# Gate and up products of one feed-forward, computed in two halves of the array's rows

## The chip, the cores and the metric

The kernel runs on one core of a Trainium2 chip. TensorE multiplies matrices on an array of 128 rows by 128 columns: one operand (the weights of the array, up to 128 x 128) is loaded, the other streams through, and the products are added into a bank of PSUM (128 partitions x 512 fp32). VectorE and ScalarE read PSUM and work on data in SBUF; GpSimd does a few small things; SyncE issues the transfers from HBM. The metric is device time in microseconds (us) of one execution.

## The reference

A trunk of two layers works on 256 tokens of 1,024 features, in fp32. Each layer is a feed-forward, a token mixer that runs in parallel with a cross-attention, and a second feed-forward, each followed by a layer norm over `alpha * x + sublayer(x)`:

```python
for l in range(DEPTH):
    x = layer_norm(alpha * x + 0.5 * swiglu(x, ffn_w_gate[l, 0], ...), ...)
    ...                                    # mixer and cross-attention
    x = layer_norm(alpha * x + mix, ln_g[l, 1], ln_b[l, 1])
    x = layer_norm(alpha * x + 0.5 * swiglu(x, ffn_w_gate[l, 1], ...), ...)

def swiglu(x, w_gate, w_up, w_down):
    return (jax.nn.silu(x @ w_gate) * (x @ w_up)) @ w_down
```

The hidden width is 2,816. So there are four feed-forwards; the change concerns the second one, that is the one that ends the first layer: l = 0, j = 1 in the code.

## The kernel before

Every fp32 operand of a large product is split into a high and a low part of type fp32r (a shorter float that TensorE takes in one pass): `split` (L101, L102) copies the raw weights to `wh` on ScalarE and subtracts on VectorE to get `wl`. A product is then three matmuls: high by high, high by low, low by high.

A feed-forward (`ffn`) goes through 11 groups of 256 hidden features. The weights of a group's gate and up matrices come in two pieces of 128 x 2048, each with 4 of the 8 chunks `k` of 128 input features; per chunk there are 256 gate columns and then 256 up columns. All four feed-forwards but the first do the first two groups in another way than the rest (`xs_groups` = 2):

- `gu_xs` (groups 0 and 1, once for each half `t` of the tokens): the activations are the loaded operand and the weights stream, 512 columns at a time. For each of 8 chunks `mm3` (L183, L184, L185) adds three matmuls into one bank `gx`. Silu on ScalarE and a multiplication on VectorE read the bank; the result is transposed by `hx` (L355) and split into the high and low `h`. During the second call, after chunk 5, the eight transposes `xt` of the layer norm ahead (`pending`) are issued, which the second half of the tokens needs.
- `gu_ws` (groups 2 to 10): the weights are the loaded operand and the activations stream. For each half `fc` of a group and each of gate and up (`m`) a bank `gu` is filled by `mmw` (L191): per chunk, `wh` with high and low activations in one matmul of 512 columns (two halves of the bank), and `wl` with the high ones in a matmul of 256. `comb` (L195, L196) then adds the two halves of the bank with a copy on ScalarE and an add on VectorE; Silu (L322), the multiplication (L323) and the split into `h` (L326, L327) follow.

The third step is `down`: `mm3` with `h` loaded and the down weights streaming, into the four banks `y`. The down product of group g - 1 stands behind the gate and up products of group g; after group 2 come those of groups 0 and 1 together; those of groups 8, 9 and 10 stand at the end, in `tail`, because the layer norm follows there by halves.

PSUM has eight banks. Four go to `y` (and other long sums), four rotate for all the rest (`mbank`): gate and up products, transposes `xt` and `hx`. A bank is given out in the order of the program, the fourth after a given one is the same bank again, and a matmul into it waits until its last reader is done.

The transfers stand on SyncE's queue in the order of the list `pieces`, three raw buffers ahead at most, and five pairs of `wh`, `wl` exist. Engines take their instructions in the order in which they are laid out, which follows the program with some matmuls moved.

Elsewhere the kernel has matmuls on part of the array: the scores of the cross-attention (`sc`, L485) work on 64 rows each, two of them one after the other with different rows and banks, in plain fp32. The projections `qkp` (L448 to L450) are fp32r matmuls of the whole array with 256 columns.

Of the kernel before, what the change touches and what calls it, by code (L numbers as in the profile page):

```python
# [8 lines left out]
F32 = mybir.dt.float32  # L9
F32R = mybir.dt.float32r  # L10
AF = mybir.ActivationFunctionType
ALU = mybir.AluOpType
AX = mybir.AxisListType

P = 128
T = 256
D = 1024
KC = D // P
# [13 lines left out]
def trunk(ctx: ExitStack, tc: tile.TileContext, d, out):  # L32
    nc = tc.nc
    pe, act, dve, pool = nc.tensor, nc.scalar, nc.vector, nc.gpsimd
# [3 lines left out]
    wp = ctx.enter_context(tc.tile_pool(name="wp", bufs=5))  # L38
# [9 lines left out]
    def ybank(name):  # L48
        return psy.tile([P, 512], F32, tag="y", name=name)

    def mbank(name):
        return psm.tile([P, 512], F32, tag="mm", name=name)

    def tmp(name):
        return tp.tile([P, 512], F32, tag="t", name=name)
# [4 lines left out]
    def downs_after(g, xs):  # L60

        if g < max(xs, 1) or g > NG - TAIL:
            return []
        return list(range(g)) if g == xs else [g - 1]
# [74 lines left out]
    def get(*key):  # L139
        while state["next"] < len(pieces) and state["next"] <= state["used"] + 1:  # L140
            trace_piece()
        assert pieces[state["used"]][0] == key, (pieces[state["used"]][0], key)
        state["used"] += 1
        return made.pop(key)
# [16 lines left out]
    for k in range(KC):  # L161
        q, o = (k, 0) if k < 2 else (1 + k // 2, k % 2 * CH)
        nc.sync.dma_start(xw[q][:, o:o + CH], d["xw"][:, k * CH:(k + 1) * CH])
        h, l = first[k // 4]
        s = slice((k % 4) * 512, (k % 4) * 512 + 512)
        split_act(xw[q][:, o:o + T], x0, k, 1)
        split(xw[q][:, o + T:o + CH], h[:, s], l[:, s])
    cur = {"x": x0}
# [10 lines left out]
    def mm3(o, a, b, start, stop):  # L179

        ah, al = a
        bh, bl = b
        pe.matmul(o, ah, bh, start=start, stop=False)  # L183
        pe.matmul(o, ah, bl, start=False, stop=False)  # L184
        pe.matmul(o, al, bh, start=False, stop=stop)  # L185

    def mmw(bank, w, a, k):

        for part in ((0, 1), (1, 0))[k % 2]:
            o, b = (bank[:, :T], a[:, 0]) if part else (bank, a.rearrange("p c t -> p (c t)"))  # L190
            pe.matmul(o, w[part], b, start=(k, part) == (0, 0), stop=(k, part) == (KC - 1, 0))  # L191

    def comb(o, bank):

        act.activation(o, bank[:, T:], AF.Copy)  # L195
        dve.tensor_add(o, o, bank[:, :T])  # L196

    HALVES = (slice(0, 64), slice(64, 128))
# [6 lines left out]
    def tsl(t):  # L205
        return slice(t * P, (t + 1) * P)

    def xpart(k, t):
        return cur["x"][:, k, 0, tsl(t)], cur["x"][:, k, 1, tsl(t)]
# [79 lines left out]
    def ffn(l, j, xs_groups, i, last=False):  # L289
        hT = {}  # L290
        y = {}

        def new_h(g):
            hT[g] = hp.tile([P, 2, 2, T], F32R, tag="h", name=f"h{l}{j}_{g}")

        def gu_ws(g, outer=False):
            w = [get("gu", l, j, g, 0), get("gu", l, j, g, 1)]
            new_h(g)
            banks = {}

            def mm(fc, m, k):
                if k == 0:
                    bank = ybank if outer and g == 0 else mbank
                    banks[fc, m] = bank(f"gu{l}{j}_{g}_{fc}{m}")
                c0 = (k % 4) * 512 + m * 256 + fc * P
                wk = w[k // 4]
                mmw(banks[fc, m], (wk[0][:, c0:c0 + P], wk[1][:, c0:c0 + P]), cur["x"][:, k], k)

            if outer:
                for k in range(KC):  # L310
                    for fc in range(2):
                        for m in range(2):
                            mm(fc, m, k)
            for fc in range(2):
                t_ = tmp(f"s{l}{j}_{g}_{fc}")
                for m in range(2):
                    if not outer:
                        for k in range(KC):
                            mm(fc, m, k)
                    comb(t_[:, m * 256:(m + 1) * 256], banks[fc, m])  # L320
                    if m == 0:
                        act.activation(t_[:, :256], t_[:, :256], AF.Silu)  # L322
                dve.scalar_tensor_tensor(t_[:, 256:], t_[:, :256], 0.5, t_[:, 256:],  # L323
                                         op0=ALU.mult, op1=ALU.mult)
                hh = hT[g][:, 0, fc, :]
                act.activation(hh, t_[:, 256:], AF.Copy)  # L326
                dve.tensor_sub(hT[g][:, 1, fc, :], t_[:, 256:], hh.bitcast(F32))  # L327

        xsw = {}

        def gu_xs(g, t, mid=None):
            if t == 0:
                xsw[g] = [get("gu", l, j, g, 0), get("gu", l, j, g, 1)]
                new_h(g)
            w = xsw[g]
            b = mbank(f"gx{l}{j}_{g}_{t}")
            for k in range(KC):
                wk = w[k // 4]
                s = slice((k % 4) * 512, (k % 4) * 512 + 512)
                mm3(b, xpart(k, t), (wk[0][:, s], wk[1][:, s]), k == 0, k == KC - 1)  # L340
                if k == 5 and mid:
                    mid()
            t_ = tmp(f"sx{l}{j}_{g}_{t}")
            act.activation(t_[:, :256], b[:, :256], AF.Silu)
            dve.scalar_tensor_tensor(t_[:, 256:], t_[:, :256], 0.5, b[:, 256:],
                                     op0=ALU.mult, op1=ALU.mult)

            def rest():
                hx(g, t, t_)
            return rest  # L350

        def hx(g, t, t_):
            tb = mbank(f"hx{l}{j}_{g}_{t}")
            for fc in range(2):
                pe.transpose(tb[:, fc * P:(fc + 1) * P], t_[:, 256 + fc * P:256 + (fc + 1) * P], ident)  # L355
            tv = tb[:, :256].rearrange("p (c t) -> p c t", c=2)
            hh = hT[g][:, 0, :, tsl(t)]
            act.activation(hh, tv, AF.Copy)
            dve.tensor_sub(hT[g][:, 1, :, tsl(t)], tv, hh.bitcast(F32))

        def down(g, t, hs, w):
            for fc in range(2):
                a = (hT[g][:, 0, fc, tsl(t)], hT[g][:, 1, fc, tsl(t)])
                for h in hs:
                    if (t, h) not in y:
                        y[t, h] = ybank(f"y{l}{j}_{t}{h}")
                    s = slice(fc * D + 512 * h, fc * D + 512 * h + 512)
                    mm3(y[t, h], a, (w[0][:, s], w[1][:, s]), g == 0 and fc == 0,
                        g == NG - 1 and fc == 1)

        late = []
        for t in range(2):
            for g in range(xs_groups):
                late.append(gu_xs(g, t, pending if (t, g) == (0, xs_groups - 1) else None))
                if len(late) > 2:
                    late.pop(0)()
                    late.pop(0)()
        for g in range(NG):
            if g == 2:
                if i == 0:  # L380
                    late_loads()
                gb = load_ln(i)
            if g >= xs_groups:
                gu_ws(g, outer=(l, j) == (0, 0) and g < 2)
                while late:
                    late.pop(0)()
            for q in downs_after(g, xs_groups):
                w = get("wd", l, j, q)
                for t in range(2):
                    down(q, t, (0, 1), w)  # L390
        nx = None if last else new_act(f"x{i}")
        ws = {g: get("wd", l, j, g) for g in range(NG - TAIL, NG)}

        def tail(t):
            for h in range(2):
                if last and (t, h) == (1, 1):
                    break
                for g in range(NG - TAIL, NG):
                    down(g, t, (h,), ws[g])
                ln_half(i, t, h, y[t, h])  # L400
            else:
                return
            down(NG - TAIL, t, (1,), ws[NG - TAIL])
            y2 = mbank("ylast")[:, :256]
            ends = [(g, fc) for g in range(NG - TAIL + 1, NG) for fc in range(2)]
            for q, o in enumerate((y[1, 1][:, :256], y2)):
                for n, (g, fc) in enumerate(ends):
                    s = slice(fc * D + 512 + 256 * q, fc * D + 768 + 256 * q)
                    mm3(o, (hT[g][:, 0, fc, tsl(t)], hT[g][:, 1, fc, tsl(t)]),
                        (ws[g][0][:, s], ws[g][1][:, s]), (q, n) == (1, 0), n == len(ends) - 1)  # L410
            ln_close(i, t, y[1, 1], y2)
        norm_both(i, gb, nx, tail)
# [420 lines left out]
    o = OutProj(0, mix, 1)  # L833
# [63 lines left out]
```

## Time and profile before

| | us |
|---|---|
| median of 3 runs (987.28 to 988.73) | 988.04 |
| the profiled execution | 987.03 |
| its span, first to last instruction | 984.9 |
| TensorE busy with matmuls in the span | 973.0 |
| VectorE busy | 663.1 |
| ScalarE busy | 528.8 |
| granted clock of TensorE, mean | 0.996 |

In rows of single instructions the columns are the start in us from the span's begin, the length in us, the engine, the line of the kernel, the operation, the tile written and the tiles read, the shape and the count; a row with a count above one goes from the first start to the last end. Shapes such as 64*128 are rows by columns of the array that are used, and 64x256 the streamed operand. A matmul's length goes from its start to its last result, so that successive matmuls overlap: the pace is read from start to start. PEld is the load of weights.

### The profile page before, as it was taken

Reading aid. Unit: us, or ns where it says so; the run is one execution under the profiler, and the core shown is the slowest. Engines: PE = TensorE matmul, PEld = TensorE weight load, DVE = VectorE, ACT = ScalarE, POOL = GpSimd, SP = SyncE. Lnnn points to the kernel's source line nnn. Section 1 sums busy time; section 2 is a strip of 40 time slices with the busy share of each in tenths; the row PEclk is TensorE's granted clock in tenths of the full one; section 3 lists DMA queues with packets and bytes.
Section 4 is the critical chain, followed back from the end, with each engine's and each line's share of the span. In section 5 each row is a group of like instructions: output and inputs, shape, how many; then the busy total and the mean of one; then the engine's idle time right before and its main releaser. Section 6 shows DMA issues by size and latency. Waiting matters only on the chain.

```text
span 984.9 us, 13270 instructions
## 1 busy us (share of the span) xinstructions
PE 973.0 (99%) x5276; PEld 832.0 (84%) x5276; DVE 663.1 (67%) x1013; ACT 528.8 (54%) x847; POOL 20.0 (2%) x31
## 2 busy tenths in 40 slices
PE   9999999999999999999999999999989999999997
PEld 8888888888888888888888888889988788888885
DVE  7676566868677656565865656577877687556565
ACT  7565555457535555555355555535874346455550
POOL 0000000000000000000000000001000000000000
PEclk9999999999999999999999999999999999999999
DMA  9784646466435654645474545434734446546421
GB/s 323 282 316 152 226 155 231 167 231 221 173 132 203 236 202 155 230 148 194 171 257 171 209 177 202 173 113 163 265 111 151 179 159 239 202 158 218 168 86 43
DMA packets 28141, 186.91 MB, mean 190 GB/s; under 512 B 3504, under 2 KB 3504, under 8 KB 7216
## 3 DMA queue, kind: packets, MB, share of 16 engines
q1 hardware_dynamic: 27792, 185.55, 52.4%
q8 instruction: 41, 0.67, 0.3%
q10 hardware_dynamic: 288, 0.52, 0.1%
q14 instruction: 20, 0.16, 0.0%
HBM read 185.01 MB, written 1.05 MB: 189 GB/s over the span
## 4 chain that ended last, share of the span: by engine, by line
PE 95%; DVE 2%; ACT 1%; DMA 1%; issue 1%; SPq 0%; DVEq 0%; ACTq 0%
PE gu L191 43%; PE y L183 8%; PE y L185 8%; PE y L184 8%; PE gx L183 2%; PE gx L185 2%; PE gx L184 2%; PE cb L191 2%; PE cx L191 2%; PE cg L191 2%; PE yo L183 2%; PE yo L185 1%; PE yo L184 1%; PE kb L191 1%; PE xt L255 1%; PE qkp L448 1%
## 5 line engine op out<-in xcount | busy, mean ns | idle before, releaser
L102 DVE TENSOR_TENSOR wl<-raw,wh 128x1024 fp32r<-128x1024 f32 x334 | 395.0, 1208 | 145.8 <-ACT wh L101 144.7
L191 PE MATMUL gu<-x,wh 128*128 128x512 f32 x1216 | 389.0, 395 | 0.0
L101 ACT ACTIVATE wh<-raw 128x1024 fp32r<-128x1024 f32 x334 | 332.8, 1042 | 97.2 <-PE y L185 28.8
L191 PEld LDWEIGHTS gu<-x,wl 128*128 128x128 f32 x1216 | 228.4, 188 | 52.3 <-DVE wl L102 1.0
L191 PE MATMUL gu<-x,wl 128*128 128x256 f32 x1216 | 243.0, 278 | 0.2 <-DVE wl L102 0.2
L191 PEld LDWEIGHTS gu<-x,wh 128*128 128x128 f32 x1216 | 189.5, 189 | 3.6 <-ACT wh L101 0.2
L183 PE MATMUL y<-wh,h 128*128 128x512 f32 (+1 forms) x352 | 137.4, 390 | 0.0
L184 PE MATMUL y<-wl,h 128*128 128x512 f32 (+1 forms) x352 | 136.6, 388 | 0.0
L185 PE MATMUL y<-wh,h 128*128 128x512 f32 (+1 forms) x352 | 136.5, 389 | 0.0
L196 DVE TENSOR_TENSOR s<-s,gu 128x256 f32<-128x256 f32 x152 | 63.1, 418 | 103.2 <-ACT s L195 103.0
L195 ACT ACTIVATE s<-gu 128x256 f32<-128x256 f32 x152 | 57.9, 382 | 104.6 <-PE gu L191 104.5
L185 PEld LDWEIGHTS y<-wh,h 128*128 128x128 f32 x352 | 66.1, 188 | 14.2 <-DVE h L327 0.4
L184 PEld LDWEIGHTS y<-wl,h 128*128 128x128 f32 x352 | 66.1, 188 | 13.6
L183 PEld LDWEIGHTS y<-wh,h 128*128 128x128 f32 x352 | 66.1, 188 | 12.9 <-ACT h L326 0.7
L326 ACT ACTIVATE h<-s 128x256 fp32r<-128x256 f32 x76 | 31.8, 418 | 66.1 <-DVE s L323 65.9
L322 ACT ACTIVATE s<-s 128x256 f32<-128x256 f32 x76 | 31.5, 416 | 37.9 <-DVE s L196 37.9
L327 DVE TENSOR_TENSOR h<-s,h 128x256 fp32r<-128x256 f32 x76 | 32.1, 422 | 17.2 <-ACT h L326 17.0
L285 ACT ACTIVATE x<-xt 128x512 fp32r<-128x512 f32 x20 | 11.4, 597 | 51.5 <-PE xt L255 51.1
L183 PE MATMUL gx<-wh,x 128*128 128x512 f32 x96 | 38.0, 396 | 0.0
L185 PE MATMUL gx<-wh,x 128*128 128x512 f32 x96 | 37.5, 392 | 0.0
L184 PE MATMUL gx<-wl,x 128*128 128x512 f32 x96 | 37.4, 390 | 0.0
L323 DVE SCALAR_TENSOR_TENSOR s<-s 128x256 f32<-128x256 f32 x76 | 32.0, 421 | 1.8 <-ACT s L322 0.5
(218 smaller groups left out, 988.9 us busy)
## 6 DMA issues: line engine op xcount, KB each, us to landing
raw<-in_wgu SPq DMA_DIRECT2D x83, 1024.0 KB, 4.8
raw<-in_wd SPq DMA_DIRECT2D x43, 1024.0 KB, 4.8
raw<-in_wconv SPq DMA_DIRECT2D x10, 1024.0 KB, 5.3
raw<-in_wout SPq DMA_DIRECT2D x8, 1024.0 KB, 4.8
raw<-in_wm SPq DMA_DIRECT2D x7, 1024.0 KB, 5.0
gb<-in_lngb SPq DMA_DIRECT2D x6, 1024.0 KB, 4.8
raw<-in_wkv SPq DMA_DIRECT2D x4, 1024.0 KB, 4.7
raw<-in_wop SPq DMA_DIRECT2D x4, 776.0 KB, 4.2
```

Source lines behind the costliest of these rows:

```text
L101: act.activation(h, raw, AF.Copy)
L102: dve.tensor_sub(l, raw, h.bitcast(F32))
L183: pe.matmul(o, ah, bh, start=start, stop=False)
L184: pe.matmul(o, ah, bl, start=False, stop=False)
L185: pe.matmul(o, al, bh, start=False, stop=stop)
L191: pe.matmul(o, w[part], b, start=(k, part) == (0, 0), stop=(k, part) == (KC - 1, 0))
L195: act.activation(o, bank[:, T:], AF.Copy)
L196: dve.tensor_add(o, o, bank[:, :T])
L322: act.activation(t_[:, :256], t_[:, :256], AF.Silu)
L323: dve.scalar_tensor_tensor(t_[:, 256:], t_[:, :256], 0.5, t_[:, 256:], op0=ALU.mult, op1=ALU.mult)
L326: act.activation(hh, t_[:, 256:], AF.Copy)
L327: dve.tensor_sub(hT[g][:, 1, fc, :], t_[:, 256:], hh.bitcast(F32))
```

## The change

In the second feed-forward alone, each matmul of the gate and up products is replaced by two, one for the upper 64 rows of the array (input features 0 to 63 of the chunk) and one for the lower 64, which add into two different banks. The two banks are added afterwards: ScalarE copies one of them to SBUF, VectorE adds the other.

In groups 2 to 10 the three products (wh by high x, wh by low x, wl by high x) are matmuls of 256 columns each, and all three add into the same 256 columns, so that gate and up of a half group stand side by side in one bank: 48 matmuls of 64 rows and 256 columns where 16 matmuls of 128 rows, half of 512 and half of 256 columns, stood. The copy and the add are of 512 columns, once per half group, in place of 256 columns each, twice. In groups 0 and 1 each of the 24 matmuls of 512 columns becomes two with 64 rows, and a second bank, a copy and an add of 512 columns come in.

```diff
+        def gu_rows(g):
+
+            w = [get("gu", l, j, g, 0), get("gu", l, j, g, 1)]
+            new_h(g)
+            for fc in range(2):
+                t_ = tmp(f"s{l}{j}_{g}_{fc}")
+                ab = [mbank(f"gr{l}{j}_{g}_{fc}{r}") for r in range(2)]
+                for m in range(2):
+                    for k in range(KC):
+                        c0 = (k % 4) * 512 + m * 256 + fc * P
+                        wk = w[k // 4]
+                        for n, (wp, xp) in enumerate(((0, 0), (0, 1), (1, 0))):
+                            for o, r in zip(ab, HALVES):
+                                pe.matmul(o[:, m * 256:(m + 1) * 256], wk[wp][r, c0:c0 + P],
+                                          cur["x"][r, k, xp], start=(k, n) == (0, 0),
+                                          stop=(k, n) == (KC - 1, 2))
+                act.activation(t_, ab[1], AF.Copy)
+                dve.tensor_add(t_, t_, ab[0])
+                act.activation(t_[:, :256], t_[:, :256], AF.Silu)
+                dve.scalar_tensor_tensor(t_[:, 256:], t_[:, :256], 0.5, t_[:, 256:],
+                                         op0=ALU.mult, op1=ALU.mult)
+                hh = hT[g][:, 0, fc, :]
+                act.activation(hh, t_[:, 256:], AF.Copy)
+                dve.tensor_sub(hT[g][:, 1, fc, :], t_[:, 256:], hh.bitcast(F32))
+
         def gu_ws(g, outer=False):
+            if (l, j) == (0, 1):
+                return gu_rows(g)
...
+            rows = (l, j) == (0, 1)
             b = mbank(f"gx{l}{j}_{g}_{t}")
+            b2 = mbank(f"gy{l}{j}_{g}_{t}") if rows else None
...
-                mm3(b, xpart(k, t), (wk[0][:, s], wk[1][:, s]), k == 0, k == KC - 1)
+                if rows:
+                    for n, (xp, wp) in enumerate(((0, 0), (0, 1), (1, 0))):
+                        for o, r in zip((b, b2), HALVES):
+                            pe.matmul(o, xpart(k, t)[xp][r], wk[wp][r, s], start=(k, n) == (0, 0),
+                                      stop=(k, n) == (KC - 1, 2))
+                else:
+                    mm3(b, xpart(k, t), (wk[0][:, s], wk[1][:, s]), k == 0, k == KC - 1)
...
             t_ = tmp(f"sx{l}{j}_{g}_{t}")
+            if rows:
+                act.activation(t_, b2, AF.Copy)
+                dve.tensor_add(t_, t_, b)
+                b = t_
```

`HALVES` is `(slice(0, 64), slice(64, 128))`.

## The prediction

> **What bounds the kernel now.** I read the page first, then the clock by core, then the chain of waits over the stage that changes (298 to 466 us), then single matmuls in order of time.
>
> ```profile
> PE   9999999999999999999999999999989999999997
> PEclk9999999999999999999999999999999999999999
> PE 95%; DVE 2%; ACT 1%; DMA 1%; issue 1%; SPq 0%; DVEq 0%; ACTq 0%
> ...
> 321.80 11.15 PE gu L191 x64
> ...
> 344.32 11.14 PE gu L191 x64
> ...
> 443.84 22.29 PE gu L191 x128
> ```
>
> The first three rows are the page's slices and its chain; the others are the chain inside the second feed-forward. TensorE is the bound there, at a clock granted in full (nines in every slice): each group of gate and up products is 64 matmuls, 11.15 or 11.14 us, without a gap. Nine groups (one of 11.15, six of 11.14, a last pair of 22.29) are 100.28 us. A group has 4 banks of 24 products of 256 columns each: today wh meets high and low x in one matmul of 512 columns, wl meets high x in one of 256. So 16 matmuls, 16 weight loads and 6,144 columns fill a bank in 2.785 us. Only the pace at which TensorE takes matmuls matters, and anything that makes it wait.
>
> **1. The pace of the new pairs.** A bank of work becomes 24 pairs of 64-row matmuls, 256 columns each. If the halves of a pair run side by side, the columns that must stream stay 6,144; but there are now 24 steps in place of 16, and each has its own weight load. So the question is the time from one pair to the next. The changed form does not occur before. Two neighbours do: whole-array matmuls of 256 columns of the same type (qkp), and pairs of 64-row halves in plain fp32 (sc).
>
> ```profile
> 701.37 0.28 PE L448 MATMUL qkp<-x,wh 128*128 128x256 f32 x1
> ...
> 704.12 0.28 PE L450 MATMUL qkp<-x,wl 128*128 128x256 f32 x1
> 704.33 1.13 PE L485 MATMUL sc<-kT,xqT 64*128 64x256 f32 x8
> 705.39 0.39 PE L448 MATMUL qkp<-x,wh 128*128 128x256 f32 x1
> 705.62 0.28 PE L449 MATMUL qkp<-x,wh 128*128 128x256 f32 x1
> ```
>
> ```profile
> L485 PE MATMUL sc<-kT,xqT x32: 376/376/480, 224.6 to 709.2; 64*128 64x256 f32 x32
> ```
>
> ```profile
> 224.94 0.60 PE L485 MATMUL sc<-kT,xqT 64*128 64x256 f32 x4
> 226.23 0.38 PE L485 MATMUL sc<-kT,xqT 64*128 64x256 f32 x2
> ```
>
> The 24 qkp matmuls start 23 steps apart in 704.12 - 701.37 = 2.75 us: 0.120 each, a weight load before every one. Two sc matmuls, each at least 0.376 long, take 0.38 together (226.23): they start within some nanoseconds of each other, so row halves with banks of their own do run side by side. From 224.94 to 226.23 are six pairs: 0.215 each. The plain fp32 pair moves its columns at half rate: 0.215 for 256, so both halves together move no more columns per microsecond than one whole-array matmul of the kernel's type. That the pair also holds at full rate is not shown.
>
> I take 0.120 for a pair, as qkp is the same type, the same size and has the same load per step. The nine groups have 9 x 96 = 864 pairs: 864 x 0.120 = 103.7, that is +3.4. The break-even is 100.28/864 = 0.116.
>
> Lower bound: the fp32 pair scaled to full rate, 0.215/2 = 0.1075: 92.9, or -7.4. Next bound: what a matmul costs beyond its columns is paid by each half.
>
> ```profile
> 298.47 0.39 PE L183 MATMUL gx<-wh,x 128*128 128x512 f32 x1
> 298.70 0.39 PE L184 MATMUL gx<-wl,x 128*128 128x512 f32 x1
> 298.92 0.39 PE L185 MATMUL gx<-wh,x 128*128 128x512 f32 x1
> ...
> 307.76 0.39 PE L185 MATMUL gx<-wh,x 128*128 128x512 f32 x1
> ```
>
> These are 42 matmuls of 512 columns, 41 steps in 9.29 us: 0.227 each. So 256 columns more cost 0.107, and 0.013 is left over in every matmul. Paid twice, a pair takes 0.133: 114.9, +14.6. Upper bound: no overlap, 0.240 a pair: 207.4, +107.
>
> The Trainium skill's TensorE: Matmul & The Clock Gate, LDWEIGHTS, speaks against the change: a load takes as long as its columns, however few its rows. The trace agrees:
>
> ```profile
> L191 PEld LDWEIGHTS gu<-x,wl 128*128 128x128 f32 x1216 | 228.4, 188 | 52.3 <-DVE wl L102 1.0
> ```
>
> ```profile
> L485 PEld LDWEIGHTS sc<-kT,xqT x32: 182/187/187, 224.6 to 709.0; 64*128 64x128 f32 x32
> ```
>
> 188 ns whole, 187 ns with 64 rows: half-height loads are no cheaper. Its model of packed matmuls (Part 3) adds about 4 ns for a second tile; my estimate by it is 0.124 a pair, +6.9 in place of +3.4. I stay with the row.
>
> **2. The two x-stationary groups (gx).** 96 matmuls of 512 columns become 96 pairs of 512. At 0.227 for either: 0. By the bounds: 0.215 a pair gives -1.2; 0.013 paid twice +1.2; no overlap 96 x 0.227 = +21.8.
>
> **3. Going from the whole array to halves and back.** From the qkp row at 704.12 to that at 705.62 are 1.50 us. Without any cost of change it would be one step of 0.120, four pairs of 0.215 (8 records) and a step of 0.120: 1.10. So there and back costs 0.40. The changed stage goes there ten times: into the first gx, back after the eight transposes in its second, back after the four of hx, and for the seven groups 3 to 9, each of which has a down product ahead of it; group 2 follows gx and group 10 follows group 9 directly. 4.0 us. A part is paid today, because going between fp32 transposes and matmuls has a gap too:
>
> ```profile
> 332.79 0.60 PE L355 MATMUL hx<-ident,sx 128*128 128x128 f32 x4
> 333.14 0.48 PE L183 MATMUL y<-wh,h 128*128 128x512 f32 x1
> 333.46 0.40 PE L184 MATMUL y<-wl,h 128*128 128x512 f32 x1
> ```
>
> Here 0.32 stands in place of 0.23. Five of the twenty passages touch transposes; I take off 0.4 and put +3.6 (0 to 4.0). The Trainium skill's TensorEngine Tiling, Key Properties, says that a change of tiling mode drains the engine; the 0.40 agrees.
>
> **4. Banks.** Four banks rotate. Each gx now holds two, and the pending transposes take two between the second and third gx. So the third's banks are the second's, just ended, and the fourth's are the third's, with two hx banks between. Today each gx takes one, and nothing waits. The release takes a copy of 512 columns on ScalarE and then an add on VectorE.
>
> ```profile
> L285 ACT ACTIVATE x<-xt 128x512 fp32r<-128x512 f32 x20 | 11.4, 597 | 51.5 <-PE xt L255 51.1
> ```
>
> ```profile
> 314.29 2.36 DVE L102 TENSOR_TENSOR wl<-raw,wh 128x1024 fp32r<-128x1024 f32 x2 [2.99 <-ACT wh L101]
> ```
>
> ```profile
> 472.27 0.69 DVE L233 SCALAR_TENSOR_TENSOR z<-xnat,y 128x512 f32<-128x512 f32 x1 [0.73 <-PE y L185]
> ```
>
> ```profile
> 315.49 0.39 PE L185 MATMUL gx<-wh,x 128*128 128x512 f32 x1
> 315.72 0.60 PE L355 MATMUL hx<-ident,sx 128*128 128x128 f32 x4
> 316.07 0.48 PE L183 MATMUL gx<-wh,x 128*128 128x512 f32 x1
> ```
>
> A gx matmul's record is 0.39 long, and its successor starts 0.23 after it: 0.16 until the bank can be read, 0.60 copy, 0.69 add, about 0.1 for the signals (an estimate): 1.55 for the third gx. Behind that wait its matmuls and all that follows on TensorE. For the fourth, the next thing on VectorE is two weight splits until 316.65; 0.69 more is 317.34. Today the third ends and hx starts at 315.72, and the four transposes cover 0.35: 1.3 us. Together +2.8 (0 if other work is set ahead; 5.2 if one split of 1.2 stands before each add).
>
> In the other groups a fresh pair of banks was last used a whole half group (5.6 us) earlier, longer than its release. The work on ScalarE and VectorE shrinks per half group (one copy and one add of 512 for two of 256 each); it is hidden under TensorE, with 107 of 170 us of VectorE busy in this stage:
>
> ```profile
> 285.00:455.00 170.00, 169.99 (x880) 144.55 (x879) 107.38 (x152) 88.59 (x135) 1.98 (x2) 1.00 0.54 192
> ```
>
> (The columns after the length are TensorE, its loads, VectorE, ScalarE and GpSimd, busy us and count.) The four gx add 0.60 and 0.69 each, hidden but for the waits above. DMAs, pieces and their order stay.
>
> **5. The end of the last group.** Today the two copies of a half group are taken as each bank ends; then both come after the second. From the last matmul to h that is 0.60 + 0.69 + 0.42 (Silu) where 0.38 + 0.42 stood: +0.9.
>
> ```profile
> L196 DVE TENSOR_TENSOR s<-s,gu 128x256 f32<-128x256 f32 x152 | 63.1, 418 | 103.2 <-ACT s L195 103.0
> L195 ACT ACTIVATE s<-gu 128x256 f32<-128x256 f32 x152 | 57.9, 382 | 104.6 <-PE gu L191 104.5
> ...
> L322 ACT ACTIVATE s<-s 128x256 f32<-128x256 f32 x76 | 31.5, 416 | 37.9 <-DVE s L196 37.9
> ```
>
> The cover is nearly used up already:
>
> ```profile
> 470.11 0.42 ACT L326 ACTIVATE h<-s 128x256 fp32r<-128x256 f32 x1 [1.12 <-DVE s L323]
> ```
>
> ```profile
> 470.27 0.39 PE L184 MATMUL y<-wl,h 128*128 128x512 f32 x1
> 470.58 0.50 PE L183 MATMUL y<-wh,h 128*128 128x512 f32 x1
> ```
>
> TensorE's step at 470.27 is 0.31 where 0.23 is usual, just behind the write of h. I take +0.5 (0 to 0.9), as some matmuls with other operands are still left to go ahead.
>
> **Sum.** 3.4 + 0 + 3.6 + 2.8 + 0.5 = +10.3. The profiled execution took 987.03 (span 984.9); 997.3. The median of the runs is 1.0 higher: 998.3.
>
> **Rivals.**
> - *The halves do not overlap at this type's full rate* (the change does not do what it says). For: the only pairs in the trace move at half rate, and their sum is exactly one full stream. Against: they do start together, and each partition would be read no faster than today. 107 + 21.8 + 6.9 (parts 3 to 5) = +136: 1124.
> - *Each half pays its own 0.013.* For: it is left over in each matmul of this type, whatever its length. Against: the fp32 pair shows no second share. 14.6 + 1.2 + 6.9 = +22.7: 1010.7.
> - *Not slower: a pair costs only its columns.* For: the fp32 pairs have almost nothing left over (0.215 for 256 columns at half rate, twice the 0.107 above). If the left-over comes from whole-array swaps of weights, which row halves hide, a pair takes 0.1075: -7.4 - 1.2 + 6.9 = -1.7: 986.3. It decides from a pair below 0.109, where 864 and 96 pairs save what parts 3 to 5 cost. If the bank waits vanish as well, 983.5.
>
> **How the numbers follow.** Forecast 0.60, no overlap 0.16, paid twice 0.12, not slower 0.12. The likeliest one's own range is 992 to 1004 (a pair of 0.116 to 0.121, parts 3 to 5 worth 4 to 11). The range 985 to 1013 takes in the second and third as well and leaves no overlap out. This kernel's measurement tells 0.2% (2 us) from no change. Faster by more: half of the last rival, 0.06. Within: the other half and a thin tail of the forecast, 0.08. Slower: 0.86.
>
> **What would show it.** Part 1: 64-row gu matmuls in twos some nanoseconds apart, a pair every 0.120; a half group alone near 5.76 us. If starts are evenly spread, there is no overlap. Part 3: about 0.1 more at the first and second step after each down product and at the first two of it. Part 4: gaps of TensorE of 1 to 2 us ahead of the third and fourth gx, released by VectorE's add. Part 5: a gap under 1 us in the last down products. A pair under 0.109 or over 0.13 makes the prediction wrong.

## The result and the profile after

The changed kernel takes 997.76 us (median of four runs, 996.28 to 998.54) against 987.82 us before: a ratio of 1.0101, with a 95% interval of 1.0087 to 1.0116. It is slower by about 10 us; the forecast was 998.3.

The profiled execution took 998.54 us, with a span of 996.4 us. These are rows of its page: the clock by slices, and the groups that take the place of the gate and up products.

```profile
PEclk9999999999999999999999999999989999999999
...
L309 PE MATMUL gr<-x,wh 64*128 64x256 f32 x1152 | 105.2, 281 | 0.0
...
L309 PE MATMUL gr<-x,wl 64*128 64x256 f32 x576 | 82.1, 280 | 0.0
```

There are 1,728 matmuls of 64 rows where 576 of 128 rows stood. The clock is granted in full in the stage that changed; the 8 in its row stands at 722 to 747 us, far behind that stage, and is taken up below. The row that sums 82.1 us for 576 matmuls of 280 ns counts overlapping time once; busy times tell little here, and the pace has to be read from start to start. These are TensorE's starts at the head of group 4, in the timeline after:

```profile
364.71 0.39 PE L185 MATMUL y<-wh,h 128*128 128x512 f32 x1
365.02 0.50 PE L309 MATMUL gr<-x,wh 64*128 64x256 f32 x4
365.36 0.28 PE L309 MATMUL gr<-x,wl 64*128 64x256 f32 x2
365.48 0.40 PE L309 MATMUL gr<-x,wh 64*128 64x256 f32 x4
365.72 0.28 PE L309 MATMUL gr<-x,wl 64*128 64x256 f32 x2
365.84 0.40 PE L309 MATMUL gr<-x,wh 64*128 64x256 f32 x4
```

From 365.36 to 365.72 run six matmuls, three pairs: 0.120 us a pair. The halves overlap at the full rate of this type. The first pair after the down product comes 0.31 after the last matmul of `y` (0.23 is usual) and holds its successors up by another 0.1: that is the change from the whole array to halves.

The chain of waits over the whole stage shows where else the time went:

```profile
316.93 0.61 ACT sx L380
317.58 0.96 PE gx L372 x3
...
338.74 0.60 DVE s L313
339.34 0.34 DVE h L398
339.73 0.50 PE y L185
...
365.09 11.70 PE gr L309 x192
376.79 0.43 PE y L183
382.45 11.70 PE gr L309 x192
...
474.74 1.01 DVE wl L102
475.88 2.35 DVE wl L102 x2
478.23 0.59 DVE s L313
478.83 1.14 DVE wl L102
479.96 0.35 DVE s L315
480.33 0.42 ACT h L318
480.80 0.50 PE y L183
```

Before, the chain stayed on TensorE all through the stage. Now it leaves TensorE in three places: ahead of the fourth `gx` (317), for the first down products (up to 339.7) and for the last ones (474 to 481). A group takes 11.70 us where 11.14 stood.

The starts of the stages on TensorE, us from the begin of each span:

| start of | before | after | later by |
|---|---|---|---|
| first gx | 298.47 | 298.73 | 0.26 (0.17 of it inherited) |
| transposes hx between third and fourth gx | 315.72 | 316.82 | 1.10 |
| hx behind group 2 | 332.79 | 335.56 | 2.77 |
| first down product | 333.14 | 335.97 | 2.82 |
| group 3 | 344.16 | 347.66 | 3.51 |
| group 4 | 360.74 | 365.02 | 4.28 |
| group 9 | 443.68 | 451.82 | 8.15 |
| last down products | 465.96 | 475.04 | 9.08 |
| transposes behind them | 478.54 | 488.54 | 10.00 |

By the start of the third feed-forward the difference is 9.94 us (483.80 and 493.73), of which 0.17 was there before the stage: the change costs 9.77 us in its own stage. The spans differ by 11.5. The other 1.6 us arise in the mixer of the second layer, which the change does not touch. There TensorE waits in `negm` (2.7 us before, 2.6 after), and about the end of that wait the granted clock falls to one half: for 3.41 us before (717.68 to 721.09), for 6.83 us after (727.09 to 733.92). These are stretches of the kernel before and then of the changed one:

```profile
717.68:721.09 3.41, 3.41 (x18) 3.41 (x17) 3.35 (x12) 2.45 (x9) 0.00 (x0) 0.50 0.00 0
721.10:724.50 3.40, 3.40 (x30) 3.40 (x30) 2.09 (x5) 2.61 (x7) 0.00 (x0) 1.00 0.66 229
```

```profile
727.10:730.50 3.40, 3.40 (x17) 2.58 (x13) 3.37 (x15) 2.44 (x10) 0.00 (x0) 0.50 0.00 0
730.50:733.90 3.40, 3.40 (x18) 3.40 (x17) 1.02 (x3) 1.21 (x5) 0.00 (x0) 0.50 0.55 159
```

(The length is followed by the busy time and count of TensorE, its loads, VectorE, ScalarE and GpSimd, then by the granted clock and the DMA.) The projections behind `negm` step about 0.21 us at the halved clock and 0.120 at the full one. The end of this text comes back to it.

### The profile page after: what moved, and what is told of

Its sections match the earlier page's. It is cut to its first block, busy times and chain, and to the rows that moved or that the text cites. A ratio compares the mean times of both kernels' runs of the same rounds, so it can differ in the third digit from the quotient of the medians.

```text
span 996.4 us, 15735 instructions
## 1 busy us (share of the span) xinstructions
PE 983.8 (99%) x6524; PEld 850.4 (85%) x6524; DVE 664.1 (67%) x999; ACT 527.8 (53%) x833; POOL 19.9 (2%) x31
## 4 chain that ended last, share of the span: by engine, by line
PE 94%; DVE 2%; ACT 2%; DMA 1%; issue 1%; DVEq 0%; ACTq 0%
PE gu L191 33%; PE gr L309 10%; PE y L183 8%; PE y L185 8%; PE y L184 8%; PE gx L372 2%; PE cb L191 2%; PE cx L191 2%; PE cg L191 2%; PE yo L183 2%; PE gx L183 1%; PE gx L185 1%; PE gx L184 1%; PE yo L185 1%; PE yo L184 1%; DVE wl L102 1%
## 5 line engine op out<-in xcount | busy, mean ns | idle before, releaser
L191 PE MATMUL gu<-x,wh 128*128 128x512 f32 x928 | 297.5, 396 | 0.0
L191 PEld LDWEIGHTS gu<-x,wl 128*128 128x128 f32 x928 | 174.7, 188 | 38.9
L191 PE MATMUL gu<-x,wl 128*128 128x256 f32 x928 | 186.4, 278 | 0.0
L191 PEld LDWEIGHTS gu<-x,wh 128*128 128x128 f32 x928 | 145.3, 189 | 3.1
L309 PE MATMUL gr<-x,wh 64*128 64x256 f32 x1152 | 105.2, 281 | 0.0
L196 DVE TENSOR_TENSOR s<-s,gu 128x256 f32<-128x256 f32 x116 | 48.0, 417 | 78.0 <-ACT s L195 77.8
L309 PEld LDWEIGHTS gr<-x,wh 64*128 64x128 f32 x1152 | 89.7, 187 | 2.5 <-issue 2.5
L195 ACT ACTIVATE s<-gu 128x256 f32<-128x256 f32 x116 | 43.8, 380 | 80.9 <-PE gu L191 80.9
L309 PE MATMUL gr<-x,wl 64*128 64x256 f32 x576 | 82.1, 280 | 0.0
L309 PEld LDWEIGHTS gr<-x,wl 64*128 64x128 f32 x576 | 55.0, 187 | 0.0
```

Source lines behind the costliest of these rows:

```text
L309: pe.matmul(o[:, m * 256:(m + 1) * 256], wk[wp][r, c0:c0 + P], cur["x"][r, k, xp], start=(k, n) == (0, 0), stop=(k, n) == (KC - 1, 2))
```

## The experiments

Times are set against runs of the kernel before on the same chip (medians 987.2 to 987.6). "In the stage" is the lateness at the start of the third feed-forward, less what stood at the start of the second, read from the traces as in the table above.

### Whole array, but 24 matmuls per bank

```diff
-    ab = [mbank(f"gr{l}{j}_{g}_{fc}{r}") for r in range(2)]
+    ab = mbank(f"gr{l}{j}_{g}_{fc}")
...
-                for o, r in zip(ab, HALVES):
-                    pe.matmul(o[:, m * 256:(m + 1) * 256], wk[wp][r, c0:c0 + P], cur["x"][r, k, xp], ...)
+                pe.matmul(ab[:, m * 256:(m + 1) * 256], wk[wp][:, c0:c0 + P], cur["x"][:, k, xp], ...)
...
-                act.activation(t_, ab[1], AF.Copy)
-                dve.tensor_add(t_, t_, ab[0])
-                act.activation(t_[:, :256], t_[:, :256], AF.Silu)
+                act.activation(t_[:, :256], ab[:, :256], AF.Silu)
...
-            rows = (l, j) == (0, 1)
+            rows = False
```

> Groups 2 to 10 with the whole array, but in 24 matmuls of 256 columns per bank as in the change (no halves, one bank per half group, Silu and the multiplication read it directly); groups 0 and 1 as before the change. Theory (the 0.12 us step is the price of 24 steps with a load each, not of halves): 864 steps of 0.120 us are 103.7 against 100.3, so +3.4 us over the kernel before (991.2), no switches of mode, and no wait at the end of the last group because the chain to h is shorter. Rival (the second half costs something in each pair, the whole array would take 256 columns in 0.115 us as wl does today): +0 us or slightly less than before.

Measured: 992.63 us, ratio 1.0045 (1.0033 to 1.0058). The chain of waits of this kernel:

```profile
344.31 11.51 PE gr L308 x96
```

96 matmuls of the whole array take 11.51 us, 0.120 each; the changed kernel's 192 halves take 11.70. The other 0.19 is the change of mode: a group of halves that follows another one directly takes 11.52 (in the run with fewer changes, below). So a pair of halves costs what one matmul of the whole array costs, and the loss of pace comes from 24 steps in place of 16. In the stage the loss is 3.5 us; the last down products start without a wait.

### Halves, but with the 16 matmuls of before

```diff
-            ab = [mbank(f"gr{l}{j}_{g}_{fc}{r}") for r in range(2)]
...
+                ab = [mbank(f"gr{l}{j}_{g}_{fc}{m}{r}") for r in range(2)]
...
-                    for n, (wp, xp) in enumerate(((0, 0), (0, 1), (1, 0))):
-                        for o, r in zip(ab, HALVES):
-                            pe.matmul(o[:, m * 256:(m + 1) * 256], wk[wp][r, c0:c0 + P], cur["x"][r, k, xp], ...)
+                    for part in ((0, 1), (1, 0))[k % 2]:
+                        for o, r in zip(ab, HALVES):       # two banks for each of gate and up
+                            oo, xx = ((o[:, :T], cur["x"][r, k, 0]) if part else
+                                      (o, cur["x"][r, k].rearrange("p c t -> p (c t)")))
+                            pe.matmul(oo, wk[part][r, c0:c0 + P], xx, ...)
...
+                act.activation(u, ab[1], AF.Copy)
+                dve.tensor_add(u, u, ab[0])
+                dve.tensor_add(t_[:, m * 256:(m + 1) * 256], u[:, :256], u[:, 256:])
```

> The change with halves of the array, but with the matmuls of 512 and 256 columns of the kernel before: 16 pairs per bank in place of 24; four quarter sums are added afterwards with two adds and one copy per bank. Groups 0 and 1 as in the change. Theory (pace goes by steps and columns, halves are free): a group of 32 double pairs takes 11.14 us as before, so the 3.4 us of the pace are gone; the switches (10 times 0.4 us), the waits in the gx part (about 1.2) and the end of the last group (0.9, perhaps 0.5 more as the chain has one add more) stay: +6 to +7 us over before (994 to 995). Rival (halves cost 0.004 us or more per pair, whatever their length): 10 us over before or more.

Measured: 999.92 us, ratio 1.0118 (1.0101 to 1.0134). The time speaks for the rival, the trace against it. The chain of waits, and then TensorE's waits in the stage (waiter, releaser, us in total, times, longest):

```profile
364.22 11.35 PE gr L311 x128
```

```profile
PEld y L183 <- ACT h L322: 2.5, 1, 2.5
PEld gr L311 <- issue: 2.5, 7, 0.4
PEld gr L311 <- DVE u L315: 1.9, 2, 1.0
```

A group takes 11.35, that is the 11.14 of before and 0.21 for the change of mode: the pace is back. Groups 3 to 8 lose 0.43 us each, not 0.77. What eats the gain is the longer chain on ScalarE and VectorE, which have twice as many banks to empty: group 10 waits for banks (1.9) and the weight load of the last down products for h (2.5); from the start of group 9 to the end of the down products 6.4 us are lost, against 1.85 in the change: 11.7 us in the stage. My expectation had the pace right and the price of two more operations per bank too low by some 5 us.

### Halves in groups 2 to 10 alone, and in groups 0 and 1 alone

```diff
-            rows = (l, j) == (0, 1)
+            rows = False
```

> Halves in groups 2 to 10 alone; groups 0 and 1 with the whole array as before. Theory: pace +3.4, eight switches there and back (one into group 2, seven into groups 3 to 9) 3.2, end of the last group 0.9: +7.5 us over before (995.3). Rival (most of the loss is in the two gx groups with their bank waits): +4 us or less.

Measured: 995.63 us, ratio 1.0079 (1.0065 to 1.0093), in the stage 7.8 us.

```diff
-            if (l, j) == (0, 1):
-                return gu_rows(g)
```

> Halves in groups 0 and 1 alone; groups 2 to 10 as before. Theory: three switches there and back 1.2, waits for banks and for h behind the longer chains 1.2 to 1.6, pace 0: +2.5 us over before (990.3). My recorded 2.8 us of bank waits alone would make it +4. Rival (halves of 512 columns cost 0.013 more per pair): +1.3 on top.

Measured: 990.45 us, ratio 1.0027 (1.0016 to 1.0038), in the stage 2.4 us. Both come out as expected, and they add up to the whole: 10.2 against 9.8, as the two alone hold eleven trips between halves and whole array, and the change ten (0.4).

### Banks of their own for groups 0 and 1

```diff
-            b2 = mbank(f"gy{l}{j}_{g}_{t}") if rows else None
+            b2 = ybank(f"gy{l}{j}_{g}_{t}") if rows else None
```

> The change, with the second bank of each of the four gx calls taken from the other four banks, which are idle there. Theory (of the 2.4 us that the gx part loses, 1.2 are switches and 1.2 waits for banks): 1 us less than the change (996.7), and the third and fourth gx start without a wait, both halves together. Rival (the waits there are for the split activations or the transposes): no gain.

Measured: 996.01 us, ratio 1.0089 (1.0072 to 1.0106), in the stage 8.5 us: 1.3 less than the change. At the head of the fourth gx, first in the changed kernel, then in this one:

```profile
317.58 0.50 PE L372 MATMUL gx<-wh,x 64*128 64x512 f32 x1
317.92 0.39 PE L372 MATMUL gx<-wl,x 64*128 64x512 f32 x1
318.15 0.39 PE L372 MATMUL gx<-wh,x 64*128 64x512 f32 x1
318.37 0.49 PE L372 MATMUL gy<-wh,x 64*128 64x512 f32 x1
318.38 0.39 PE L372 MATMUL gx<-wh,x 64*128 64x512 f32 x1
```

```profile
316.41 0.66 PE L394 MATMUL hx<-ident,sx 128*128 128x128 f32 x4
317.00 0.49 PE L372 MATMUL gx<-wh,x 64*128 64x512 f32 x1
317.00 0.49 PE L372 MATMUL gy<-wh,x 64*128 64x512 f32 x1
```

With a bank of its own the second half starts with the first; in the change it starts 0.79 us behind it. So the bank waits are real, and worth about 1.3 us. About 0.3 of it is lost in the third gx (from the first gx to the hx behind the third, 18.09 us in the change and 17.81 here) and 0.95 in the fourth and what follows (from there to the hx behind group 2, 18.74 and 17.78).

### Fewer changes between halves and whole array

```diff
+        if two and g > xs:                 # two: the second feed-forward
+            return [] if g % 2 else [g - 2, g - 1]
         return list(range(g)) if g == xs else [g - 1]
```

> The change, with the down products taken two groups at a time (after group 4 those of 2 and 3, after 6 those of 4 and 5, after 8 those of 6 and 7), so that halves and whole array alternate 7 times and not 10. Theory (0.4 us for there and back): 3 x 0.4 = 1.2 us less than the change (996.5), if the same order costs the kernel before nothing. Rival (what is lost around the down products is a wait for h or weights and not the switch): no gain, or a loss as in the whole-array kernel with the same order.

> The kernel before the change, with the same order of down products: the control for the run with halves. Theory: TensorE stays full, so the same time as before within 0.3 us. If the order itself costs or saves something (weights that come later), it shows here.

Measured: with halves 997.46 us, ratio 1.0106 (1.0091 to 1.0122); the control 987.39 us, ratio 1.0 (0.9991 to 1.0009). The time shows no gain over the change, and with intervals that reach 1.5 us to either side it could not show one of this size. In the stage the loss is 8.6 us against 9.77, about 1.1 less, near the 1.2 of three trips at 0.40, and the control loses nothing there. The chain of waits shows two groups in one stretch, where two times 11.70 stood:

```profile
347.59 23.22 PE gr L311 x384
```

The second group of a stretch takes 23.22 - 11.70 = 11.52 us, that is 96 steps of 0.120 without a change of mode. Behind the stage both profiled executions lose the same 1.6 us in the mixer, and their spans are 996.4 and 995.0. So the 0.40 is shown in the stage and not in the time.

### Last group with the whole array

```diff
-            if (l, j) == (0, 1):
+            if (l, j) == (0, 1) and g < NG - 1:
                 return gu_rows(g)
```

> The change, but group 10 with the whole array as before. Theory (the wait in the last down products is that of the longer chain behind group 10): pace of one group 0.38 and the 0.92 us of the end come back: 1.3 us less than the change (996.5). Rival (the wait there comes from weight splits that stand ahead on ScalarE and VectorE and not from the chain's length): 0.4 us less only.

Measured: 996.82 us, ratio 1.0099 (1.0083 to 1.0114), which the time alone does not part from the change. In the stage the loss is 8.7 us, 1.1 less, near the theory's 1.3 and far from the rival's 0.4. ScalarE's timeline from the first copy behind group 10 to the write of h, in the changed kernel (down products start at 475.04) and in this one (474.89):

```profile
476.51 0.57 ACT L312 ACTIVATE s<-gr 128x512 f32<-128x512 f32 x1
...
480.33 0.42 ACT L318 ACTIVATE h<-s 128x256 fp32r<-128x256 f32 x1 [1.05 <-DVE s L315]
```

```profile
475.66 0.36 ACT L195 ACTIVATE s<-gu 128x256 f32<-128x256 f32 x1
...
479.04 0.42 ACT L353 ACTIVATE h<-s 128x256 fp32r<-128x256 f32 x1 [1.11 <-DVE s L350]
```

Set against the start of the down products, the change writes h 1.14 us later (5.29 and 4.15). 0.70 of that is there already when the copy starts (1.47 and 0.77), because three weight splits stand ahead of it on ScalarE and not two; 0.44 is the longer chain (3.82 and 3.38, each with the splits that VectorE does in between). So theory and rival both hold a part: the new order of the copies lets one more split go first.

### Order of the halves

```diff
-                        for n, (wp, xp) in enumerate(((0, 0), (0, 1), (1, 0))):
-                            for o, r in zip(ab, HALVES):
+                        for o, r in zip(ab, HALVES):
+                            for n, (wp, xp) in enumerate(((0, 0), (0, 1), (1, 0))):
```

> The change with another order in groups 2 to 10: for each chunk the three products of the lower-numbered half, then the three of the other half, in place of pairs. Theory (TensorE starts matmuls in order and a half can run beside the other only when the other's matmul is next in line): of each three steps of a half, the last overlaps the first of the other half, so six matmuls take four steps of 0.120 us and not three: 288 x 0.48 = 138.2 us against 103.7, +34.6 us over the change (1032). Rival 1 (TensorE looks ahead past waiting matmuls, the halves run as two streams): no slower than the change, 998. Rival 2 (no overlap at all without neighbours): 288 x 0.72 = 207.4, +104 us, 1101.

Measured: 999.7 us (one run). My theory fell: it costs nothing, in the stage 9.7 us as in the change. The timeline:

```profile
349.02 0.41 PE L309 MATMUL gr<-x,wh 64*128 64x256 f32 x4
349.26 0.29 PE L309 MATMUL gr<-x,wl 64*128 64x256 f32 x2
349.38 0.41 PE L309 MATMUL gr<-x,wh 64*128 64x256 f32 x4
```

Each half's three products stand together in the program, also as it is laid out for TensorE, and yet they start in twos, six in 0.36 us. TensorE does start a matmul of one half ahead of earlier ones of the other. To see how far, whole blocks of 24 were tried:

```diff
+                    for o, r in zip(ab, HALVES):
+                        for k, n, wp, xp in seq:      # all 24 products of one half
+                            pe.matmul(o[:, m * 256:(m + 1) * 256], w[k // 4][wp][r, c0:c0 + P], ...)
```

> The change with all 24 products of one half of a bank's quarter sums first and then all 24 of the other half (groups 2 to 10; the run with three and three showed that a half may lag the other by three). Theory now: the two halves are queues of their own, filled in program order from one window of W matmuls. A half can start while the other still works only when its first matmul has come into the window; a block of 48 then takes 48 - 2W steps of 0.120 us, at least 24. 36 blocks: W = 2: +86 us over the change (1084), W = 8: +35 us (1033), W of 12 or more: 998. Rival (no window that small, the halves are wholly independent streams): 998.

Measured: 1076.3 us (one run). The chain of waits, and the timeline where one block ends and the other half's begins:

```profile
381.26 20.53 PE gr L310 x192
```

```profile
383.68 0.28 PE L310 MATMUL gr<-x,wl 64*128 64x256 f32 x1
383.69 0.51 PE L310 MATMUL gr<-x,wh 64*128 64x256 f32 x4
384.03 0.29 PE L310 MATMUL gr<-x,wl 64*128 64x256 f32 x2
384.14 0.40 PE L310 MATMUL gr<-x,wh 64*128 64x256 f32 x2
```

192 matmuls in 20.53 us are 171 steps of 0.120: 21 of 192 are saved. Four pairs of blocks have seven borders, so that is three at each. The timeline shows them: the six matmuls that start from 383.69 on, ahead of 384.14, are the last three of one half and the first three of the other. (The expectation's formula gives every block of 48 two borders; the last block of a group has only one: 192 - 7 x 3 = 171.) With W = 3 the formula gives 42 steps for a block of 48, 36 x 18 x 0.120 = 78 us over the change, 1076. So the look-ahead is about three matmuls, enough for the run before and far too little here.

## Why the prediction was right

*Part 1, the pace (+3.4).* Right in size and reason. Without the change of mode a group of pairs takes 0.38 more than before (11.52 against 11.14), nine of them 3.4. The 0.120 taken from the whole-array neighbour holds to the nanosecond, and the whole-array run shows that it is the price of a step. Of the bounds, the left-over of 0.013 is neither paid twice nor hidden by the halves. The 4 ns that the Trainium skill's TensorE: Matmul & The Clock Gate (Part 3) adds for a second tile do not show in the pace here: halves start some nanoseconds apart, but the steps of each stay 0.120.

*Part 2 (0).* Right: from the second pair on, the pairs of 512 columns keep 0.227 each while the halves start together.

*Part 3, the changes of mode (+3.6).* Right. Groups 3 to 8 lose 0.77 each (from 360.74 and 377.33 against 365.02 and 382.38): 0.38 is pace, 0.39 the trip. The three trips in the gx part cost about 1.0, seen undisturbed where the banks are separate; together 3.7. Seven trips in place of ten give 1.1 us back.

*Part 4, banks (+2.8).* The mechanism was right, its size wrong: about 1.3. The step that failed is "the third's banks are the second's, just ended". They are not. In TensorE's waits the second half of the third gx waits 0.2 us for VectorE's split `x`, the last reader of a bank of the transposes:

```profile
PEld gx L372 <- ACT sx L380: 0.3, 1, 0.3
PEld gy L372 <- DVE x L286: 0.2, 1, 0.2
```

As the program is built, the banks do not simply rotate: the third gx has the two banks of the transposes, which come free sooner, and not the fourth ones before it. So it lost 0.3 where 1.55 was put. The fourth has the third's two banks, as foretold; it waited for the copy and then, in its second half, for the add, up to 318.37, and lost 0.95 where 1.3 was put.

*Part 5, the end of the last group (+0.5).* Late h is what TensorE waits for, and it measured 0.92. The step that was mis-sized is "0.60 + 0.69 + 0.42 (Silu) where 0.38 + 0.42 stood: +0.9": the chain itself is longer by 0.44 only, and one more weight split ahead of it, which I had not looked for, is the larger part. Of the 1.14 by which h came later, TensorE lost 0.92: the cover that I had hoped for was 0.2 and not 0.4.

*What was not in the sum.* The first down products wait about 0.5 us for h of groups 0 and 1 (339.34 and 339.73 in the chain): the add of 512 columns of group 2 stands ahead of it on VectorE (338.74), itself behind weight splits.

Altogether 3.4 + 0 + 3.7 + 1.3 + 0.9 + 0.5 = 9.8, and the stage lost 9.77. The forecast of 10.3 came this close because the banks were put 1.5 too high, the end of the last group 0.4 too low, and the 0.5 was left out. That these errors cancel to within 0.5 us is luck; the pace and the changes of mode, 7.1 of the 9.8, are not.

The rivals: no overlap at full rate is excluded by the pairs at 0.120; paid twice and only the columns are both excluded by the same number.

## What to carry to other kernels

A full contraction cut into row halves gains nothing: the columns that stream stay the same, each step still has its own load, and a step of this type has a fixed part of 0.013 us; so count steps as well as columns. The costs around it are then the changes between halves and whole array (0.40 us there and back, so do them seldom), and the added copy and add, which hurt only where a bank or the next operand is waited for at once. A neighbouring row of the same type and size gave the price of the new form better than any scaled bound.

## What the runs showed of the hardware that was not expected

Row halves run like two queues with a short look-ahead, in contrast to the order that "The kernel before" gives for engines. A program order of three and three runs at the speed of pairs; blocks of 24 do not, with an overlap of three matmuls at each border. The half that a bank held up at 318, where the first half's first four matmuls are laid out ahead, stays three matmuls behind the other; both step on at 0.233 us in place of 0.227. At the head of group 2 the first half, now with 256 columns, has to wait for the second: its fourth matmul starts 0.23 us behind its third, where 0.12 is usual.

```profile
323.39 0.28 PE L309 MATMUL gr<-x,wh 64*128 64x256 f32 x1
...
323.51 0.39 PE L309 MATMUL gr<-x,wl 64*128 64x256 f32 x1
...
323.74 0.61 PE L309 MATMUL gr<-x,wh 64*128 64x256 f32 x4
```

The Trainium skill's TensorE: Matmul & The Clock Gate, Part 3, says that matmuls start strictly in program order; these runs show otherwise for halves with different rows.

TensorE's wait in `negm` in the second layer's mixer (1.4 to 3.3 us) and the halved clock behind it move the end of every kernel here. Up to `negm` the profiled executions keep within 0.9 us the distance that they had at the start of the third feed-forward, and behind the mixer it stays as it is. In between, the three kernels with 3.41 us at half the clock (the kernel before, halves in groups 0 and 1 alone, and the control) end up between 1.0 us ahead of the kernel before and level with it; the others, with 6.83 us or more, fall behind it by 0.9 to 3.0 us. That is more than some of the effects here, so effects of that size were read in the stage, and end to end only with the intervals. What stays open is why one execution has a longer stretch than another: each kernel has a single profiled execution, and no experiment was made on it.
